# Interleaving the two halves of stationary operands, element by element, for the 512-column matmuls of a two-layer encoder

## The chip, the cores and the metric

The kernel runs on one core of one Trainium2 chip. The metric is device time in microseconds (us) of one launch that computes both outputs. A profile of one execution stands beside the timed runs. Engine names are those of the profile: PE is the matrix engine (its matmuls), PEld the same engine's weight loads, DVE the vector engine, ACT the scalar engine, POOL the general engine, SP the queue that issues most DMAs. L599 is line 599 of the kernel before.

## The reference

Two sequences of 512 tokens with 1024 channels go through the same trunk of two layers. Everything is float32.

```python
for i in range(2):                       # layer 0: attention, layer 1: retention
    h = rms_norm(x, norm_g[i])
    proj = h @ w_in                      # layer 0: 1024 x 8192, layer 1: 1024 x 6144
    q, k, v, gate = split(proj)
    ...
    x = x + (rms_norm(mixer(q, k, v)) * silu(gate)) @ w_out     # 2048 x 1024
y = rms_norm(x, final_norm_g)
```

The attention layer has 8 heads, each with two softmaxes of 512 x 512 scores, subtracted from each other; queries and keys are rotated (rope). The retention layer has 8 heads with a decay in both directions, worked in two chunks of 256 tokens.

## The kernel before, in words

**Halves.** The matmuls take operands in a rounded 32-bit format (fp32r). To keep float32 accuracy each operand is split in two: ACT writes the rounded value (hi, `hi_of`, L399 and L400), DVE writes what is left (lo, `lo_of`, L402 and L403). A product is then three matmuls into one PSUM bank, named by `PASSES`: hi by hi, hi by lo, lo by hi. In each pair the first letter is the stationary operand (the one that PE loads as weights, 128 columns at a time), the second the moving one (streamed through, 512 or 256 columns). Every matmul has its own weight load, also where it loads the same weights as the one before. In the trace a group of three therefore shows six records.

**The input projections.** Both use a seven-product block scheme for matrix products (products P1 to P7, on sums and differences of blocks). A `Unit` covers 256 columns of the weight matrix. In a unit of kind "pair" (queries, keys, gates) the block of the weight matrix is the stationary operand: `prep` makes it (DVE sums and differences into `st`, then hi and lo into a tile of the ring `ws`, which has 7 buffers), and `product` issues 12 matmuls (4 steps of 128 channels by three passes) of 512 columns each at L599, with the moving operands `bt` from the tokens' blocks (`make_b`). In a unit of kind "wide" (values) it is the other way round: token blocks are stationary, the weight matrix moves, 256 columns at a time (L609).

**The tile that a pair product loads.** `prep` takes `ws` as `[P, 2, 4, n]`: all hi values, then all lo values. A load of step k reads 128 values that lie side by side.

**Attention.** Rotated queries and keys leave `rot_done` (its inner `store`) through a staging tile `os` of shape `[P, 2, S]` (row 0 hi, row 1 lo) to DRAM by DMA, and come back through `load_qk`. `scores` (L1104 to L1118) loads 128 queries as weights and moves 512 keys: three matmuls of 512 columns per score tile at L1116. The probabilities are transposed (L1161) and multiplied with the values in matmuls of 256 columns (L1181). `weigh` multiplies by the gate and splits the gated sums into `oT`, two slots of a large tile (`arena`), one for hi and one for lo, made by `new_oT`.

**The output projections.** `out_step` loads 128 tokens of `oT` as weights and moves 512 columns of the output matrix (from `ws`): six matmuls per step at L891. DVE adds the result to the residual (L896). Both layers use it.

**Retention.** Its scores, states and sums are matmuls of 256 columns (L1315, L1339, L1359, L1367).

**What sets the order.** A planner (`Plan`) records every operation with a cost per engine, what it reads and what it writes, simulates the five engines, and fixes one order of instructions per engine when the program is built. At run time each engine follows its list and waits on semaphores.

Of the kernel before, what the change touches and what calls it, by code (L numbers as in the profile page):

```python
# [15 lines left out]
P = 128  # L16
# [237 lines left out]
def trunk_kernel(  # L254
# [45 lines left out]

    arena = ar.tile([P, 18 * 1024 + 80], F32R, tag="arena", name="arena")

    def slot(n, shape, dt=F32R, shift=0):

        size = math.prod(shape[1:])
        at = None if n in (12, 13) or n >= 20 else n if n < 12 else n - 2
        if at is None:
            assert not shift  # L310
            cnt[0] += 1
            label = f"b_{cnt[0]}"
            return Buf(plan, f"b{n}", 1, lambda i: cp.tile(shape, dt, tag=f"b{n}", name=label))
        assert dt == F32R
        lo = 32 + at * 1024 + shift

        def make(i):
            t = arena[:, lo:lo + size]
            return t.rearrange("p (a b) -> p a b", a=shape[1]) if len(shape) == 3 else t
        b = Buf(plan, f"b{n}", 1, make)  # L320
        b.also = Buf(plan, f"edge{at + 1 if shift else at}", 1, None)
        return b
# [195 lines left out]
    class Unit:  # L518
# [32 lines left out]
        def prep(self, op):  # L551
            x = self.take
            n = 256 if self.wide else P

            def combine(a, b, fn):
                t = st_t([P, 4, n])
                out = ((lambda: self.like(t.t)), t)
                dve(4 * n, lambda: nc.vector.tensor_tensor(out[0](), a[0](), b[0](), op=fn), [a[1], b[1]], [t])
                return out
            if op == "P1":  # L560
                src = x(0, 0)
            elif op == "P2":
                src = x(0, 1)
            elif op == "P4":
                src = x(1, 1)
            elif op == "P5":
                src = self.s[1] = combine(x(1, 0), x(1, 1), ALU.add)
            elif op == "P6":
                src = self.s[2] = combine(self.s[1], x(0, 0), ALU.subtract)
            elif op == "P3":  # L570
                src = combine(x(0, 1), self.s[2], ALU.subtract)
            else:
                src = combine(x(0, 0), x(1, 0), ALU.subtract)
            if self.wide:
                a, b = ws_t([P, 4, n]), ws_t([P, 4, n])
                hi, lo = ((lambda: a.t), a), ((lambda: b.t), b)
            else:
                s = ws_t([P, 2, 4, n])
                hi, lo = ((lambda: s[:, 0]), (s, 0)), ((lambda: s[:, 1]), (s, 1))
            hi_of(4 * n, lambda: self.like(hi[0]()), src[0], [src[1]], [hi[1]])  # L580
            lo_of(4 * n, lambda: self.like(lo[0]()), src[0], lambda: self.like(hi[0]()), [src[1], hi[1]], [lo[1]])
            self.ops[op] = (hi, lo)
            if op == "P2" and self.early is not None:
                self.early, self.x = None, {}
# [75 lines left out]
                self.done(1, 0, X, s, True)  # L660


    def rot_done(dst, tab, scaled, turned=None):

        cos, sin = tab

        def mul(out, a, t, psum):
            if scaled:  # L670
                dve(S, lambda: nc.vector.scalar_tensor_tensor(out.t, a.t, SC, t.t, op0=ALU.mult, op1=ALU.mult),
                    [a, t], [out])
            elif psum:
                dve(S, lambda: nc.vector.tensor_tensor(out.t, a.t, t.t, op=ALU.mult), [a, t], [out])
            else:
                dve(S, lambda: nc.vector.tensor_tensor(out.t, a.t, t.t, op=ALU.mult), [a, t], [out])

        def store(g, i, r):
            o = os_t()
            hi_of(S, lambda: o[:, 0, :], lambda: r.t, [r], [(o, 0)])  # L680
            lo_of(S, lambda: o[:, 1, :], lambda: r.t, lambda: o[:, 0, :], [r, (o, 0)], [(o, 1)])
            for j in range(2):
                dma(lambda j=j: dst[g][j, i * 64:(i + 1) * 64], lambda j=j: o[j * 64:(j + 1) * 64].bitcast(F32),
                    [o], [(dst[g], (i, j))], 256)

        def done(i, g, tiles, s, psum):
            x = tiles[0]
            if i == 0:
                s["b0", g] = x
                return  # L690
            a, m1, m2 = s["b0", g], m_t(), m_t()
            mul(m1, a, cos, False)
            mul(a, a, sin, False)
            mul(m2, x, sin, psum)
            if psum:
                m3 = m_t()
                mul(m3, x, cos, psum)
            else:
                m3 = x
                mul(x, x, cos, psum)  # L700
            dve(S, lambda: nc.vector.tensor_tensor(m1.t, m1.t, m2.t, op=ALU.subtract), [m1, m2], [m1])
            store(g, 0, m1)
            dve(S, lambda: nc.vector.tensor_tensor(a.t, a.t, m3.t, op=ALU.add), [a, m3], [a])
            store(g, 1, a)
            if turned:
                turn(g, m1, a)

        def turn(g, *r):
            h, to = turned
            out = [m_t("kt"), m_t("kt")]  # L710
            for i in range(2):
                tp = bank("tp", "ktp")

                def fn(i=i, tp=tp):
                    for t in range(NT):
                        nc.tensor.transpose(tp[:, t * P:(t + 1) * P], r[i][:, t * P:(t + 1) * P], ident.t)
                pe(0.44, fn, [r[i], ident], [tp], 2)
                for j in range(2):
                    dve(256, lambda i=i, j=j, tp=tp: nc.vector.tensor_tensor(
                        out[j].t.rearrange("p (t i c) -> p t i c", t=NT, i=2)[:, :, i, :],  # L720
                        tp.t.rearrange("p (t j c) -> p t j c", t=NT, j=2)[:, :, j, :],
                        powers[:, h + j, :].unsqueeze(2).broadcast_to([P, NT, 64]), op=ALU.mult),
                        [tp, powers], [(out[j], i)])
            for j in range(2):
                o, k = os_t(), out[j]
                hi_of(S, lambda o=o, k=k: o[:, 0, :], lambda k=k: k.t, [k], [(o, 0)])
                lo_of(S, lambda o=o: o[:, 1, :], lambda k=k: k.t, lambda o=o: o[:, 0, :], [k, (o, 0)], [(o, 1)])
                dma(lambda j=j: to[h + j, g].rearrange("a p c -> p a c"), lambda o=o: o.t.bitcast(F32),
                    [o], [to[h + j, g]], 512)
        return done  # L730
# [66 lines left out]
    def weigh(y, sg, oT, c, scale=1.0):  # L797


        here = slice(c * 256, (c + 1) * 256)  # L800
        og, sq = c_t("og"), m_t("sq")
        wide = lambda t: t.rearrange("p (e n) -> p e n", e=2)
        dve(S, lambda: nc.vector.tensor_tensor(wide(og.t), wide(y.t), sg[:, :, here], op=ALU.mult), [y, sg], [og])
        hi_of(S, lambda: oT[0][:, :, here], lambda: wide(og.t), [og], [(oT[0], c)])
        lo_of(S, lambda: oT[1][:, :, here], lambda: wide(og.t), lambda: oT[0][:, :, here], [og, (oT[0], c)],
              [(oT[1], c)])
        act(S, lambda: nc.scalar.activation(sq.t, y.t, AF.Square, scale=scale), [y], [sq])
        dve(256, lambda: nc.vector.tensor_tensor(sq[:, 0:256], sq[:, 0:256], sq[:, 256:512], op=ALU.add), [sq], [sq])
        return sq
# [14 lines left out]
        return rr  # L824

    def new_oT(g):
        return [slot(16 + 2 * g + a, [P, 2, S], F32R, 32) for a in range(2)]

    def load_qk(src, i, shift):
        t = slot(i, [P, 2, S], F32R, shift)  # L830
# [129 lines left out]

    def units1(tab):
        ropes = [Unit(w1, which * DI + h * 256, "pair",
                      rot_done({g: qk_d[0, which, h, g] for g in range(NG)}, tab, which == 0), half_view)
                 for h in range(NH) for which in range(2)]
        gates = [Unit(w1, 3 * DI + h * 256, "pair", gate_done({g: g_d[0, h, g] for g in range(NG)}, 16))
                 for h in range(NH)]
        wides = [Unit(w1, 2 * DI + h * 256, "wide",
                      v_done({(i, g): v_d[0, h + i, g] for i in range(2) for g in range(NG)}))
                 for h in range(0, NH, 2)]
        return mixed(ropes, gates, wides, 2, 5)  # L970
# [136 lines left out]
    def scores(i):  # L1107
        h, g, t = tiles[i]
        st[i]['s'] = []
        for j in range(2):  # L1110
# [2 lines left out]

            def fn(s=s, q=q, k=k):
                for n, (a, b) in enumerate(PASSES):
                    nc.tensor.matmul(s.t, q[:, a, t * P:(t + 1) * P], k[:, b, :], start=(n == 0), stop=(n == 2))  # L1116
            pe(0.7, fn, [q, k], [s])
            st[i]['s'].append(s)  # L1118

# [414 lines left out]
```

## Time and profile before

| | |
|---|---|
| time, median of 3 runs | 1809.73 us (1808.83 to 1810.48) |
| span of the profiled execution, first to last instruction | 1807.0 us |
| median over that span | 2.7 us more |
| granted PE clock, mean | 0.999 |
| POOL busy | 169.5 us (9%) |
| DMA | 328.81 MB moved, mean 182 GB/s |

The profile gives no time of its own for the profiled execution beside the span; the 2.7 us between span and median is taken as what lies around the span. "Busy" is the union of an engine's instructions in time, so that it never exceeds the span. In the groups of instructions a row gives the line, engine, operation, the written tile and the read tiles, the count, the busy time, the mean duration of one record, and the idle time ahead of them. Matmuls are pipelined: a record runs from its start until its results are written, and neighbours overlap, so the mean of one is longer than the distance from one to the next. That distance (the pitch) is found by dividing a stretch of time by the matmuls in it.

### The profile page before, as it was taken

Reading aid. Unit: us, or ns where it says so; the run is one execution under the profiler, and the core shown is the slowest. Engines: PE = TensorE matmul, PEld = TensorE weight load, DVE = VectorE, ACT = ScalarE, POOL = GpSimd, SP = SyncE. Lnnn points to the kernel's source line nnn. Section 1 sums busy time; section 2 is a strip of 40 time slices with the busy share of each in tenths; the row PEclk is TensorE's granted clock in tenths of the full one; section 3 lists DMA queues with packets and bytes.
Section 4 is the critical chain, followed back from the end, with each engine's and each line's share of the span. In section 5 each row is a group of like instructions: output and inputs, shape, how many; then the busy total and the mean of one; then the engine's idle time right before and its main releaser. Section 6 shows DMA issues by size and latency. Waiting matters only on the chain.

```text
span 1807.0 us, 27780 instructions
## 1 busy us (share of the span) xinstructions
PE 1794.9 (99%) x10299; PEld 1558.1 (86%) x10299; DVE 1477.1 (82%) x2319; ACT 895.1 (50%) x1856; POOL 169.5 (9%) x323
## 2 busy tenths in 40 slices
PE   9999999999999999999999999999999999999998
PEld 6789889898988888888888888898989898888887
DVE  7958787778699888888888897787887967888887
ACT  7753444433434565554555866444434355444346
POOL 1000000000000022222322300000000000111113
PEclk9999999999999999999999999999999999999999
DMA  6444455555545685444554524464657559765662
GB/s 217 134 126 137 161 140 178 184 168 155 174 126 175 201 334 198 178 156 159 190 204 140 190 73 146 140 210 146 205 156 228 151 170 396 272 238 182 225 218 94
DMA packets 162767, 328.81 MB, mean 182 GB/s; under 512 B 12724, under 2 KB 76872, under 8 KB 162632
## 3 DMA queue, kind: packets, MB, share of 16 engines
q1 hardware_dynamic: 162304, 326.71, 54.1%
q8 instruction: 81, 1.33, 0.3%
q14 instruction: 54, 0.44, 0.1%
q10 hardware_dynamic: 328, 0.34, 0.1%
HBM read 209.55 MB, written 117.44 MB: 181 GB/s over the span
## 4 chain that ended last, share of the span: by engine, by line
PE 93%; DVE 2%; DMA 2%; ACT 2%; issue 1%; POOL 0%; SPq 0%; POOLq 0%; DVEq 0%; ACTq 0%
PE pj L599 20%; PE pj L891 19%; PE sc L599 10%; PE pj L609 10%; PE o L599 8%; PE o L1181 5%; PE sc L1116 5%; PE sc L609 5%; PE o L609 2%; PE o L1359 2%; PE tp L1161 2%; PE sc L1315 1%; PE o L1367 1%; PE tp L1339 1%; DMA raw<-in_ret_w_out_dram 1%
## 5 line engine op out<-in xcount | busy, mean ns | idle before, releaser
L891 PE MATMUL pj<-ws,arena 128*128 128x512 f32 x1542 | 391.2, 397 | 0.0
L891 PEld LDWEIGHTS pj<-ws,arena 128*128 128x128 f32 x1542 | 277.7, 188 | 52.7
L599 PE MATMUL pj<-b,ws 128*128 128x512 f32 x1080 | 265.0, 392 | 0.0
L599 PEld LDWEIGHTS pj<-b,ws 128*128 128x128 f32 x1080 | 201.4, 188 | 43.0
L403 DVE TENSOR_TENSOR ws<-st,ws 128x512 fp32r<-128x512 f32 (+1 forms) x192 | 147.9, 774 | 74.8 <-ACT ws L400 56.7
L896 DVE SCALAR_TENSOR_TENSOR b<-pj,crr,b 128x512 f32<-128x512 f32 (+1 forms) x257 | 189.9, 744 | 21.4 <-PE pj L891 21.0
L403 DVE TENSOR_TENSOR ws<-raw,ws 128x512 fp32r<-128x512 f32 (+1 forms) x164 | 141.5, 868 | 71.3 <-ACT ws L400 61.0
L400 ACT CAST ws<-st 128x512 fp32r<-128x512 f32 (+1 forms) x192 | 132.4, 693 | 121.4 <-PE pj L599 36.4
L599 PE MATMUL sc<-arena,ws 128*128 128x512 f32 x768 | 186.8, 392 | 0.0
L599 PE MATMUL o<-arena,ws 128*128 128x512 f32 x744 | 180.0, 393 | 1.1 <-ACT m L385 0.6
L599 PEld LDWEIGHTS sc<-arena,ws 128*128 128x128 f32 x768 | 144.0, 188 | 31.3
L400 ACT CAST ws<-raw 128x512 fp32r<-128x512 f32 (+1 forms) x164 | 125.7, 772 | 87.0 <-PE o L599 45.0
L599 PEld LDWEIGHTS o<-arena,ws 128*128 128x128 f32 x744 | 138.4, 188 | 31.7 <-DVE arena L463 1.4
L599 PE MATMUL pj<-arena,ws 128*128 128x512 f32 x648 | 160.3, 392 | 0.4 <-DVE arena L463 0.4
L599 PEld LDWEIGHTS pj<-arena,ws 128*128 128x128 f32 x648 | 120.8, 188 | 26.7 <-DVE arena L463 0.7
L1134 ACT ACTIVATE b<-sc,nm 128x512 f32<-128x512 f32 x128 | 88.0, 689 | 66.9 <-DVE nm L1124 66.5
L636 ACT COPY c<-pj 128x512 f32<-128x512 f32 x104 | 60.9, 586 | 119.7 <-PE pj L599 66.4
L609 PE MATMUL pj<-ws,b 128*128 128x256 f32 x960 | 116.8, 276 | 0.0
L609 PEld LDWEIGHTS pj<-ws,b 128*128 128x128 f32 x960 | 113.2, 188 | 0.7
L1116 PE MATMUL sc<-arena 128*128 128x512 f32 x384 | 101.2, 395 | 0.3 <-ACT b L1134 0.3
L1181 PEld LDWEIGHTS o<-arena 128*128 128x128 f32 x768 | 93.1, 188 | 2.7
L1181 PE MATMUL o<-arena 128*128 128x256 f32 x768 | 93.7, 278 | 0.0
(207 smaller groups left out, 2855.9 us busy)
## 6 DMA issues: line engine op xcount, KB each, us to landing
qk<-os SPq DMA_DIRECT2D x192, 256.0 KB, 3.6
arena<-qk SPq DMA_DIRECT2D x96, 512.0 KB, 5.8
raw<-in_da_w_in_dram SPq DMA_DIRECT2D x64, 512.0 KB, 5.1
v<-os SPq DMA_DIRECT2D x64, 512.0 KB, 4.3
arena<-v SPq DMA_DIRECT2D x64, 512.0 KB, 4.1
raw<-in_ret_w_in_dram SPq DMA_DIRECT2D x48, 512.0 KB, 4.8
os<-g SPq DMA_DIRECT2D x32, 512.0 KB, 7.4
g<-e SPq DMA_DIRECT2D x48, 256.0 KB, 4.6
```

Source lines behind the costliest of these rows:

```text
L400: act(n, lambda: nc.scalar.copy(dst(), src()), r, w)
L403: dve(n, lambda: nc.vector.tensor_tensor(dst(), src(), hi().bitcast(F32), op=ALU.subtract), r, w)
L599: nc.tensor.matmul(ps.t, a[u][0]()[:, k, :], bt[k][:, v, :], start=(opens and k == 0 and i == 0), stop=(k == 3 and i == 2), skip_group_che ...
L609: nc.tensor.matmul(ps[:, (t % 2) * 256:(t % 2) * 256 + 256], bt[k][:, v, t * P:(t + 1) * P], a[u][0]()[:, k, :], start=(opens and t % 2 == ...
L636: act(S, lambda c=c, ps=ps: nc.scalar.copy(c.t, ps.t), [ps], [c])
L891: nc.tensor.matmul(ps[:, here], o[a][:, e, t * P:(t + 1) * P], u[b][:, e, here], start=(m == 0), stop=(m == 5))
L896: axpy(n, lambda half=half, here=here, ps=ps: nc.vector.scalar_tensor_tensor(half, ps[:, here], rr[:, t % 2:t % 2 + 1], half, op0=ALU.mult ...
L1116: nc.tensor.matmul(s.t, q[:, a, t * P:(t + 1) * P], k[:, b, :], start=(n == 0), stop=(n == 2))
L1134: act(840, lambda j=j, s=s, m=m: nc.scalar.activation(p[:, j, :], s.t, AF.Exp, bias=m.t, accum_out=sm[:, 2 * j + n:2 * j + n + 1]), [s, m] ...
L1161: nc.tensor.transpose(tp[:, j * P:(j + 1) * P], p[:, 0, j * P:(j + 1) * P], ident.t)
L1181: nc.tensor.matmul(o[:, e * 256:(e + 1) * 256], v[b][:, j, e * P:(e + 1) * P], aT[a][:, j, :], start=(n == 0), stop=(n % 12 == 11), skip_g ...
L1359: nc.tensor.matmul(o[:, e * 256:(e + 1) * 256], v_[v][:, 2 * c + j, e * P:(e + 1) * P], a_[:, u, j * 256:(j + 1) * 256], start=(e == 0 and ...
```

## The change

Three kinds of stationary operand get another place for hi and lo. They no longer stand in two blocks but alternate, element by element: hi of column 0, lo of column 0, hi of column 1, and so on. A load of 128 hi values then reads every second element over a stretch of 1024 bytes, not 128 neighbours over 512 bytes. The three are the weights of pair products (`prep`), the gated sums (`new_oT`, `weigh`), and the queries of attention (`store`, `scores`). They are just those that a matmul of 512 columns loads. The moving operands and all operands of 256-column matmuls stay as they are. ACT and DVE now write these halves with a step of two elements, and DVE reads hi with that step when it works out lo. The two slots of a gated sum become one stretch, so writing hi counts as a write to both.

```diff
+    def twin(t):
+        return t.rearrange("p a s -> p (a s)").rearrange("p (s u) -> p s u", u=2)
...
-                s = ws_t([P, 2, 4, n])
-                hi, lo = ((lambda: s[:, 0]), (s, 0)), ((lambda: s[:, 1]), (s, 1))
+                s = ws_t([P, 4, n, 2])
+                hi, lo = ((lambda: s[:, :, :, 0]), (s, 0)), ((lambda: s[:, :, :, 1]), (s, 1))
...
-    def rot_done(dst, tab, scaled, turned=None):
+    def rot_done(dst, tab, scaled, turned=None, twins=False):
...
-            hi_of(S, lambda: o[:, 0, :], lambda: r.t, [r], [(o, 0)])
-            lo_of(S, lambda: o[:, 1, :], lambda: r.t, lambda: o[:, 0, :], [r, (o, 0)], [(o, 1)])
+            part = (lambda a: twin(o.t)[:, :, a]) if twins else (lambda a: o[:, a, :])
+            hi_of(S, lambda: part(0), lambda: r.t, [r], [(o, 0)])
+            lo_of(S, lambda: part(1), lambda: r.t, lambda: part(0), [r, (o, 0)], [(o, 1)])
...
-        hi_of(S, lambda: oT[0][:, :, here], lambda: wide(og.t), [og], [(oT[0], c)])
+        hi_of(S, lambda: oT[0][:, :, here], lambda: wide(og.t), [og], [(oT[0], c), (oT[1], c)])
...
     def new_oT(g):
-        return [slot(16 + 2 * g + a, [P, 2, S], F32R, 32) for a in range(2)]
+        both = [slot(16 + 2 * g + a, [P, 2, S], F32R, 32) for a in range(2)]
+        lo = 32 + 32 + (14 + 2 * g) * 1024
+        for a, b in enumerate(both):
+            b.make = lambda i, a=a: arena[:, lo:lo + 2048].rearrange("p (e s u) -> p e s u", e=2, u=2)[:, :, :, a]
+        return both
...
-                      rot_done({g: qk_d[0, which, h, g] for g in range(NG)}, tab, which == 0), half_view)
+                      rot_done({g: qk_d[0, which, h, g] for g in range(NG)}, tab, which == 0, None, which == 0),
+                      half_view)
...
-                    nc.tensor.matmul(s.t, q[:, a, t * P:(t + 1) * P], k[:, b, :], start=(n == 0), stop=(n == 2))
+                    nc.tensor.matmul(s.t, twin(q.t)[:, t * P:(t + 1) * P, a], k[:, b, :], start=(n == 0), stop=(n == 2))
```

## The prediction

> **What bounds the kernel now.** I read the page first, then the list of waits, then the groups of one engine with shapes kept apart, then single stretches. On the page: the span, PE's busy time, and who stands in the chain that ended last.
>
> ```profile
> span 1807.0 us, 27780 instructions
> ...
> PE 1794.9 (99%) x10299; PEld 1558.1 (86%) x10299; DVE 1477.1 (82%) x2319; ACT 895.1 (50%) x1856; POOL 169.5 (9%) x323
> ...
> PE 93%; DVE 2%; DMA 2%; ACT 2%; issue 1%; POOL 0%; SPq 0%; POOLq 0%; DVEq 0%; ACTq 0%
> ```
>
> PE's records cover 99% of the span and PE is 93% of the chain. The waits of PE's matmuls, eight rows in all, of which these are the first and the last, come to about 5 us (1.4 down to 0.2 each).
>
> ```profile
> PE sc L1010 <- DVE minus L411: 1.4, 1, 1.4
> ...
> PE tp L815 <- DVE b L403: 0.2, 1, 0.2
> ```
>
> So nothing is to be had from another engine; the time is the number of matmuls times their pitch. These groups are all the 512-column matmuls that the change touches (columns after the bar: busy us, mean ns of one record, idle).
>
> ```profile
> L891 PE MATMUL pj<-ws,arena 128*128 128x512 f32 x1530 | 389.8, 398 | 0.0
> L599 PE MATMUL pj<-b,ws 128*128 128x512 f32 x1080 | 265.0, 392 | 0.0
> L599 PE MATMUL sc<-arena,ws 128*128 128x512 f32 x768 | 186.8, 392 | 0.0
> L599 PE MATMUL o<-arena,ws 128*128 128x512 f32 x744 | 180.0, 393 | 1.1 <-ACT m L385 0.6 <-DVE arena L463 0.3
> L599 PE MATMUL pj<-arena,ws 128*128 128x512 f32 x648 | 160.3, 392 | 0.4 <-DVE arena L463 0.4
> ...
> L1116 PE MATMUL sc<-arena 128*128 128x512 f32 x384 | 101.2, 395 | 0.3 <-ACT b L1134 0.3
> ...
> L599 PE MATMUL sc<-b,ws 128*128 128x512 f32 x120 | 29.1, 391 | 0.0
> ```
>
> The counts add up to 5274 of PE's 10299 records. Their pitch I take from a stretch with nothing but L599, and beside it a stretch with nothing but 256-column matmuls (L609); columns: PE, PEld, DVE, ACT, POOL busy with counts, granted clock, DMA share, GB/s.
>
> ```profile
> 62.00:150.00 88.00, 88.00 (x386) 72.18 (x386) 67.08 (x106) 50.47 (x85) 0.00 (x0) 1.00 0.43 132
> 163.50:190.60 27.10, 27.10 (x241) 27.10 (x240) 19.25 (x29) 12.03 (x20) 0.00 (x0) 1.00 0.56 172
> ```
>
> A window also counts records that reach into it, one or two here. 88.00 us over 384.5 is 229 ns per 512-column matmul; 27.10 us over 239 is 113.4 ns per 256-column one. At a full clock, then, 5274 x 229 ns = 1208 us, two thirds of the span, is what this change can speed up or slow down. In the second stretch PEld has no gap, so a load of 128 neighbouring values takes at most 113 ns of the load path; in the first it is free for 15.8 of 88 us.
>
> **The change part by part.** The built programs hold the same instructions in the same order on all five engines, before and after, the DMAs included; only 17 lo subtractions lose a wait for PE, because the hi copy ahead of them now makes it. So the planner moves nothing, no queue is passed, and everything lies in how fast the same instructions read and write.
>
> *ACT and DVE.* Pair products are 3360 matmuls (the five L599 rows) at 12 each, 280; with 64 gated sums and 32 query stores that is 376 hi copies and 376 lo subtractions. No row shows a write with a step of two. The nearest rows are reads with that step: in the second layer's rotated units a block of the weight matrix is read so. First all such groups by name, then a stretch in which every copy and subtraction from `raw` reads in steps of two.
>
> ```profile
> L400 ACT CAST ws<-st 128x512 fp32r<-128x512 f32 x160 | 98.7, 621 | 74.9 <-PE pj L599 30.3 <-issue 13.1 <-PE sc L599 11.1
> ```
>
> ```profile
> L403 DVE TENSOR_TENSOR ws<-st,ws 128x512 fp32r<-128x512 f32 x160 | 108.9, 685 | 56.7 <-ACT ws L400 56.2
> ```
>
> ```profile
> L403 DVE TENSOR_TENSOR ws<-raw,ws 128x512 fp32r<-128x512 f32 x3 | 2.1, 689 | 3.2 <-ACT ws L400 3.2
> L400 ACT CAST ws<-raw 128x512 fp32r<-128x512 f32 x3 | 2.0, 651 | 1.4 <-PE sc L599 1.4
> ```
>
> ACT pays 651 - 621 = 30 ns, DVE 689 - 685 = 4 ns. As an estimate for writes: 376 x 30 ns = 11 us more on ACT, which is busy half the time, and 376 x 4 ns = 1.5 us on DVE. What hides them is PE's own backlog: it waits 5 us in the whole run. Without that cover they would cost at most 13 us together. Below nothing they can't go by more than those 5 us. I take 0.
>
> *The loads themselves.* No row shows a load in steps of two. The largest group of loads now:
>
> ```profile
> L891 PEld LDWEIGHTS pj<-ws,arena 128*128 128x128 f32 x1542 | 277.7, 188 | 52.7
> ```
>
> The step matters in two ways: how long the load takes, and what it does to the matmul that streams beside it. For the length, one end is no change; the other is twice, 226 ns, since twice the bytes are spanned. Even that fits the 229 ns pitch by 3 ns. It would only be seen at the head of a run, where a matmul waits for its own load:
>
> ```profile
> L891 PE MATMUL pj<-ws,arena 128*128 128x512 f32 x1 | 0.5, 477 | 0.0
> ```
>
> That is one head, 477 ns where a steady record has 392: 85 ns of waiting. L891's mean of 398 says (398 - 392) x 1530 / 85 = 108 heads, L1116's 395 another 14. At 113 ns more each, a doubled load costs 122 x 113 ns = 14 us. I take no change.
>
> For the neighbour, the trace has a matmul that ran with no load beside it: the load path was idle for 0.57 us until 50.27, while the second of these two matmuls streamed from 49.73 on.
>
> ```profile
> 49.73 1.04 PE L599 MATMUL o<-arena,ws 128*128 128x512 f32 x2
> 50.27 0.19 PEld L599 LDWEIGHTS o<-arena,ws 128*128 128x128 f32 x1 [0.57 <-DVE arena L463]
> ```
>
> ```profile
> L599 PE MATMUL o<-arena,ws 128*128 128x512 f32 x1 | 0.4, 388 | 0.0
> ```
>
> It took 388 ns, where records with a load beside them take 391 to 393. I read the 4 ns as what a load and a stream cost each other when they want the same part of SBUF. The two walk at different speeds now: the stream passes 2048 bytes per partition in 229 ns, 8.9 bytes per ns, a load 512 bytes in 113 ns, 4.5. Whatever their start, they fall in and out of step. With a step of two a load passes 1024 bytes in 113 ns, 9.1 bytes per ns: the stream's own speed. Side by side at a constant distance, they either never want the same place or always do. The tiles' places put every such load 64 bytes off its stream, counted modulo 128, and a load starts with its neighbour's stream, so I take "never".
>
> The sum: 4 ns x 5274 = 21 us (the same 4 ns for L891 and L1116, whose means hold the heads). 1807.0 - 21 = 1786 us of span, 2.7 us around it as in the median of the runs: **1789 us**. What is late next is still PE.
>
> [...]
>
> **The rivals.**
> 1. *No contention to remove.* The 4 ns come from something else (the end of a run, say), and the load has slack as it is. Speaking for it: 388 is one record of its kind, and the pitch is the same 229 ns whichever tiles are read. The time is 1810 us, with up to 4 more for ACT's 11 us where its results are awaited. [...]
> 2. *Always in step, on the wrong side.* The constant distance is one at which load and stream collide at each line, for instance because the load's data are asked for earlier or later than its record starts. Now they meet about half of the time for 4 ns; always would be 8: +21 us, 1831 us, spread over L599, L891 and L1116 alike. It decides as soon as the colliding share is over a half. Against it: the 64 bytes.
> 3. *A longer load.* At twice its length 1824 us, by the heads alone (L891). From 229 ns on, 2.02 times the present length, every matmul waits: each further 10 ns cost 53 us. Against it: on ACT and DVE the step of two cost 5% and 1%, not 100%.
> [...]
>
> **How the numbers follow.** Forecast (never in step) 0.42; rival 4 0.10; rival 1 0.16; rival 2 0.22; rival 3 0.10, of which 0.04 lie beyond a doubled load. Faster by over 0.2% (about what a measurement of this kernel can tell from no change, 3.6 us) 0.52, within it 0.16, slower 0.32. The forecast's own range is 1782 to 1800. With both signs likely, the whole range reaches from 1765, some way into what lies between the forecast and rival 4, to just over rival 2, 1835: left out are most of rival 4 and the far part of rival 3, about 0.15.
>
> **What would show it.** Right: in a pure L599 stretch the pitch falls from 229 to 225 ns, the records' mean from 392 to 388, the 256-column stretch stays at 113.4 ns, and PE's waits stay near 5 us. Rival 1: 392 stays. Rival 2: 396 and a pitch of 233. Rival 3: PEld's mean above 188 ns, heads above 477. [...] ACT's copies at about 650 ns would confirm the side cost; DVE subtractions far above 689 ns, with new DVE rows among PE's waits, would show that I hid too much. A change of the 256-column pitch would put the whole picture in doubt, since no operand of theirs is touched.

## The result and the profile after

The changed kernel takes 1841.38 us (median of 5 runs, 1840.45 to 1841.5) against 1809.73: a ratio of 1.0175, 95% interval 1.0162 to 1.0187. It is slower, on the other side of the forecast of 1789, and 6.4 us above the upper end of the range. Three lines from the page of the changed kernel: the span, the busy times, the chain that ended last.

```profile
span 1839.5 us, 27771 instructions
...
PE 1827.6 (99%) x10299; PEld 1607.6 (87%) x10299; DVE 1480.1 (80%) x2319; ACT 907.6 (49%) x1856; POOL 170.4 (9%) x323
...
PE 93%; DMA 3%; DVE 2%; ACT 1%; issue 0%; POOL 0%; SPq 0%; POOLq 0%
```

The picture is as before: as many matmuls, 99% of the span, 93% of the chain. PE is busy 32.7 us longer and the span is 32.5 us longer. PE waits for nobody more than before: of its eight waits by line, these are the first and the last (total, times, longest, in us), and all eight come to 4.5 us.

```profile
PE sc L1021 <- DVE minus L415: 1.4, 1, 1.4
...
PE sc L1127 <- ACT b L1145: 0.3, 1, 0.3
```

So the same matmuls in the same order run at a longer pitch. The groups of 512-column matmuls (L603, L901 and L1127 were L599, L891 and L1116):

```profile
L901 PE MATMUL pj<-ws,arena 128*128 128x512 f32 x1530 | 394.2, 401 | 0.0
L603 PE MATMUL pj<-b,ws 128*128 128x512 f32 x1080 | 269.4, 396 | 0.0
L603 PE MATMUL sc<-arena,ws 128*128 128x512 f32 x768 | 190.1, 396 | 0.0
L603 PE MATMUL o<-arena,ws 128*128 128x512 f32 x744 | 183.2, 397 | 1.1 <-ACT m L389 0.6 <-DVE arena L467 0.3
L603 PE MATMUL pj<-arena,ws 128*128 128x512 f32 x648 | 163.1, 396 | 0.4 <-DVE arena L467 0.3
...
L1127 PE MATMUL sc<-arena 128*128 128x512 f32 x384 | 102.4, 398 | 0.3 <-ACT b L1145 0.3
```

Each mean is 3 to 4 ns above its old one (398, 392, 392, 393, 392, 395). That much the prediction had as its second rival. But the 256-column matmuls, of which no operand was touched, are slower as well; first before, then after.

```profile
L609 PE MATMUL pj<-ws,b 128*128 128x256 f32 x960 | 116.8, 276 | 0.0
...
L609 PE MATMUL sc<-ws,arena 128*128 128x256 f32 x768 | 89.6, 276 | 0.0
...
L1359 PE MATMUL o<-arena 128*128 128x256 f32 x384 | 48.9, 276 | 0.0
```

```profile
L613 PE MATMUL pj<-ws,b 128*128 128x256 f32 x960 | 120.9, 281 | 0.0
...
L613 PE MATMUL sc<-ws,arena 128*128 128x256 f32 x768 | 93.1, 281 | 0.0
...
L1370 PE MATMUL o<-arena 128*128 128x256 f32 x384 | 50.3, 280 | 0.0
```

Two stretches of the changed kernel, one with nothing but L603 and one with nothing but L613 (PE, PEld, DVE, ACT, POOL with counts, clock, DMA share, GB/s):

```profile
62.00:150.00 88.00, 88.00 (x379) 73.55 (x378) 65.43 (x104) 49.93 (x82) 0.00 (x0) 1.00 0.42 130
168.00:193.00 25.00, 25.00 (x214) 25.00 (x213) 16.25 (x25) 10.07 (x16) 0.00 (x0) 1.00 0.47 151
```

Counted as in the prediction, 88.00 us over 377.5 is 233 ns (it was 229), and 25.00 us over 212 is 118 ns (it was 113.4), both at a full clock. From here on a pitch is the distance from the end of one matmul's record to the end of the next, averaged over a group without the gaps at its heads; "sum" is the sum of all these distances in a group, gaps included. Both are taken from the trace's records. By them the span's growth divides so:

| group | matmuls | sum before, us | sum after, us | more | pitch, ns |
|---|---|---|---|---|---|
| pair products, 512 columns | 3360 | 772.7 | 787.0 | 14.3 | 229.0 to 233.3 |
| output projections, 512 | 1530 | 353.0 | 357.4 | 4.4 | 230.6 to 233.5 |
| attention's scores, 512 | 384 | 89.1 | 90.3 | 1.2 | 230.0 to 233.1 |
| wide products, 256 (untouched) | 2688 | 305.4 | 316.0 | 10.6 | 113.6 to 117.6 |
| attention's and retention's other matmuls, 256 (untouched) | 1728 | 199.4 | 202.5 | 3.1 | |

The 512-column groups give 19.9 us, the untouched ones 13.7; matmuls of 128 columns give back 0.5. The sum, 33.1 us, is the growth of the distance from the first matmul after the warm-up to the last (1788.5 to 1821.5 us); the warm-up itself was 0.6 us shorter, which leaves the span's 32.5.

### The profile page after: what moved, and what is told of

It is laid out like the page before. It is cut to its first block, busy times and chain, and to the rows that moved or that the text cites. A ratio compares the mean times of both kernels' runs of the same rounds, so it can differ in the third digit from the quotient of the medians.

```text
span 1839.5 us, 27771 instructions
## 1 busy us (share of the span) xinstructions
PE 1827.6 (99%) x10299; PEld 1607.6 (87%) x10299; DVE 1480.1 (80%) x2319; ACT 907.6 (49%) x1856; POOL 170.4 (9%) x323
## 4 chain that ended last, share of the span: by engine, by line
PE 93%; DMA 3%; DVE 2%; ACT 1%; issue 0%; POOL 0%; SPq 0%; POOLq 0%
PE pj L603 20%; PE pj L901 19%; PE sc L603 11%; PE pj L613 10%; PE o L603 8%; PE sc L613 5%; PE o L1192 5%; PE sc L1127 5%; PE o L613 2%; PE o L1370 2%; PE tp L1172 2%; PE o L1378 1%; PE sc L1326 1%; PE tp L1350 1%; DMA raw<-in_ret_w_out_dram 1%; DMA raw<-in_da_w_in_dram 1%
## 5 line engine op out<-in xcount | busy, mean ns | idle before, releaser
L901 PE MATMUL pj<-ws,arena 128*128 128x512 f32 x1542 | 395.6, 400 | 0.0
L901 PEld LDWEIGHTS pj<-ws,arena 128*128 128x128 f32 x1542 | 288.2, 195 | 46.8
L603 PE MATMUL pj<-b,ws 128*128 128x512 f32 x1080 | 269.4, 396 | 0.0
L603 PEld LDWEIGHTS pj<-b,ws 128*128 128x128 f32 x1080 | 209.1, 195 | 40.0
L404 ACT CAST ws<-st 128x512 fp32r<-128x512 f32 (+1 forms) x192 | 138.6, 726 | 134.9 <-PE pj L603 41.0
L603 PE MATMUL sc<-arena,ws 128*128 128x512 f32 x768 | 190.1, 396 | 0.0
L603 PE MATMUL o<-arena,ws 128*128 128x512 f32 x744 | 183.2, 397 | 1.1 <-ACT m L389 0.6
L404 ACT CAST ws<-raw 128x512 fp32r<-128x512 f32 (+1 forms) x164 | 129.6, 796 | 94.0 <-PE o L603 42.4
L603 PEld LDWEIGHTS sc<-arena,ws 128*128 128x128 f32 x768 | 149.5, 195 | 29.2
L603 PEld LDWEIGHTS o<-arena,ws 128*128 128x128 f32 x744 | 143.6, 195 | 29.6 <-DVE arena L467 1.3
L603 PE MATMUL pj<-arena,ws 128*128 128x512 f32 x648 | 163.1, 396 | 0.4 <-DVE arena L467 0.3
L603 PEld LDWEIGHTS pj<-arena,ws 128*128 128x128 f32 x648 | 125.4, 195 | 24.9 <-DVE arena L467 0.6
L613 PE MATMUL pj<-ws,b 128*128 128x256 f32 x960 | 120.9, 281 | 0.0
L613 PEld LDWEIGHTS pj<-ws,b 128*128 128x128 f32 x960 | 117.1, 189 | 0.6
L1127 PE MATMUL sc<-arena 128*128 128x512 f32 x384 | 102.4, 398 | 0.3 <-ACT b L1145 0.3
```

The lines of the kernel that those rows point to most:

```text
L404: act(n, lambda: nc.scalar.copy(dst(), src()), r, w)
L603: nc.tensor.matmul(ps.t, a[u][0]()[:, k, :], bt[k][:, v, :], start=(opens and k == 0 and i == 0), stop=(k == 3 and i == 2), skip_group_che ...
L613: nc.tensor.matmul(ps[:, (t % 2) * 256:(t % 2) * 256 + 256], bt[k][:, v, t * P:(t + 1) * P], a[u][0]()[:, k, :], start=(opens and t % 2 == ...
L901: nc.tensor.matmul(ps[:, here], o[a][:, e, t * P:(t + 1) * P], u[b][:, e, here], start=(m == 0), stop=(m == 5))
L1127: nc.tensor.matmul(s.t, twin(q.t)[:, t * P:(t + 1) * P, a], k[:, b, :], start=(n == 0), stop=(n == 2))
```

## The experiments

The reference time of each set is the kernel before on the same chip, 1808.56 to 1809.95 us. A distance below is the first byte of the weights that a load reads, less the first byte of the stream in progress (the next matmul's weights beside the present matmul's moving operand), in bytes of a partition counted modulo 512. It comes from the addresses in the built program. The pair products of both kernels stand at 192, which is the prediction's 64 modulo 128.

### One part at a time

`e1_pair` interleaves the weights of pair products alone, `e2_sums_queries` the gated sums and the queries alone.

```diff
-                s = ws_t([P, 2, 4, n])
-                hi, lo = ((lambda: s[:, 0]), (s, 0)), ((lambda: s[:, 1]), (s, 1))
+                s = ws_t([P, 4, n, 2])
+                hi, lo = ((lambda: s[:, :, :, 0]), (s, 0)), ((lambda: s[:, :, :, 1]), (s, 1))
```

> Only the weights of pair products are interleaved (L599, 3360 matmuls); gated sums and queries stay in blocks. Theory A (the load): a load in steps of two costs the matmul that streams beside it about 4.3 ns, wherever such a load runs and nowhere else; the slower 256-column matmuls are an after-effect of the state in which a run of them is entered. Then the pure L599 stretch has a pitch of 233.3 ns against 228.9, L891 and L1116 keep theirs, and the time is 1809.7 + 14.3 = 1824 us, up to 1836 if the 256-column runs of the projections fall into the slow state too. Theory B (the writes): stepped writes of ACT and DVE slow all of PE's reads while they run; with 280 of 376 such writes the time is about 1833 us, and L891 and L1116 are slower where such writes run beside them.

> The complement: gated sums and queries interleaved, pair products' weights in blocks. Theory A: L891 and L1116 go to a pitch of about 233.3 ns (from 230.6 and 230.0), 1530 x 2.9 + 384 x 3.1 = 5.6 us more, 1815 us, and the projections' 256-column runs keep 113.4 ns; L599 stays at 228.9. Theory B: 96 of 376 writes, about a quarter of the loss, 1818 us, and the projections keep their time.

e1 took 1832.82 us, 1.0125 (1.0108 to 1.0142); e2 took 1817.23 us, 1.0040 (1.0027 to 1.0054). Together that is 23.7 + 8.1 = 31.8 us, the whole loss of the changed kernel (31.7 us). In e1 only the pair products go to 233.3 ns; output projections and scores stay at 230.6 and 230.2. In e2 it is the other way round: 233.5 and 233.2, pair products at 229.05. So the 512-column part follows the loads that are changed, and only these. The 256-column part doesn't: in e1 the wide products are at 117.2 ns, in e2 at 113.7, but there the retention's untouched matmuls (L1359 and L1367 of before) are at 117.6 and 117.7.

### The writes or the loads

The change alters the way the halves are written and the way they are loaded. `e5_writes` writes them interleaved, as e1 does, but loads 128 neighbours; `e6_loads` writes blocks, as before, and loads every second element.

```diff
-                            ps.t, a[u][0]()[:, k, :], bt[k][:, v, :], ...
+                            ps.t, load(k, u), bt[k][:, v, :], ...
# e5, on an interleaved ws:      at = 256 * k + 128 * u;  load = w[:, at:at + 128]
# e6, on a ws in two blocks:     at = 256 * k + u;        load = w[:, at:at + 255:2]
```

> Pair products' weights are written interleaved by ACT and DVE as in e1_pair, but each load reads 128 neighbouring elements, so it mixes hi and lo of 64 columns: these products are not the reference's. Theory A: pitch 228.9 ns, time 1810 us within 3. Theory B: the time of e1_pair, 1824 to 1836 us.

> The reverse: written in blocks as before, but each load of a pair product reads every second element over 1024 bytes, so it mixes channels: these products are not the reference's. Theory A: the pitch and the time of e1_pair, 1824 to 1836 us. Theory B: 1810 us within 3.

e5: 1810.22 us, 1.0001 (0.9992 to 1.0011). e6: 1833.2 us, 1.0126 (1.0106 to 1.0146). A matmul group and a load group of e5, then the same of e6:

```profile
L606 PE MATMUL pj<-b,ws 128*128 128x512 f32 x1080 | 265.0, 392 | 0.0
```

```profile
L606 PEld LDWEIGHTS pj<-b,ws 128*128 128x128 f32 x1080 | 201.5, 188 | 43.0
```

```profile
L606 PE MATMUL pj<-b,ws 128*128 128x512 f32 x1080 | 269.4, 396 | 0.0
```

```profile
L606 PEld LDWEIGHTS pj<-b,ws 128*128 128x128 f32 x1080 | 209.1, 195 | 40.0
```

With interleaved writes and plain loads nothing changes; with plain writes and stepped loads everything of e1 is there. The writes are out: it is the load. Its own record grows from 188 to 195 ns, and the matmul beside it from 392 to 396.

### Is it the load's length?

`e8_step4`, `e12_step3` and `e11_step0` load in steps of four, three and none (one element, 128 times).

```diff
# e8:   at = 512 * (k % 2) + 2 * (k // 2) + u;  load = w[:, at:at + 509:4]
# e12:  at = 128 * k + u;                       load = w[:, at:at + 382:3]
# e11:  at = 512 * u + 128 * k;                 load = w[:, at:at + 1].broadcast_to([P, 128])
```

> Weights in blocks as before, but the loads of pair products read every fourth element over 2048 bytes; they mix halves and channels, so these products are not the reference's. Theory A2: the extra of 4.3 ns grows with the stretch touched: twice as many bytes again, so 229 + 4.3 + 8.6 = 242 ns, and a mean load record near 209 ns, 1809 + 13 x 3.36 = 1853 us and up to 12 more by the wide runs. Theory A1: the load now walks at twice the stream's speed and falls out of step, so the pitch falls back to about 229.

> Weights in blocks, loads of pair products in steps of three elements (12 bytes); they mix halves and channels, so these products are not the reference's. [...]

> Weights in blocks as before, but each load of a pair product reads one and the same element 128 times (step 0); these products are not the reference's. It measures what a load of 128 neighbours costs the stream at all. The prediction's step (a lone matmul took 388 ns, one with a load beside it 392): if a load's reads collide with the stream, a load that touches one place only brings the pitch to about 225 ns, 1809 - 13 = 1796 us. If the 4 ns were not a collision: 229 ns and 1809 us.

They took 1846.61, 1831.2 and 1816.19 us (one run each). The load group of e8, of e12 and of e11:

```profile
L606 PEld LDWEIGHTS pj<-b,ws 128*128 128x128 f32 x1080 | 265.9, 312 | 0.1
```

```profile
L606 PEld LDWEIGHTS pj<-b,ws 128*128 128x128 f32 x1080 | 254.8, 252 | 0.1
```

```profile
L606 PEld LDWEIGHTS pj<-b,ws 128*128 128x128 f32 x1080 | 201.6, 188 | 45.1
```

| step of the load | 0 | 1 | 2 | 3 | 4 |
|---|---|---|---|---|---|
| load record, ns | 188 | 188 | 195 | 252 | 312 |
| pitch of pair products, ns | 231.3 | 229.0 | 233.3 | 235.4 | 239.6 |
| wide products, ns | 113.5 | 113.6 | 117.5 | 113.6 | 113.6 |

Length does count where it is long: at steps of three and four the load path has no gap left (0.1 us idle). At two it has (40.0 us), and the pitch is 4.3 ns up nevertheless, so length is not the reason there.

e11 speaks against the forecast's own reason, without settling it. A load of one element, 128 times, stays at one place, and the pitch is 231.3 ns, above the 229.0 of the plain load, where the forecast's reason had led me to expect 225. But the stream still passes that place, and only one place was tried.

### Is it the place?

`e7_flip` moves e1's stepped loads by 64 bytes, later for the first three steps, earlier for the last; `e10_flip_blocks` does the same with plain loads. `e17_sweep_blocks` and `e18_sweep_step2` give each of the seven products a place of its own. All of them load other values than the product wants.

```diff
# e7:   at = 256 * k + u + (16 if k < 3 else -16);        load = w[:, at:at + 255:2]
# e10:  at = 512 * u + 128 * k + (16 if k < 3 else -16);  load = w[:, at:at + 128]
# d = dict(P1=0, P2=16, P5=32, P6=64, P3=80, P7=96, P4=112)[op]
# e17:  at = 512 * u + 128 * min(k, 2) + d;               load = w[:, at:at + 128]
# e18:  at = 256 * min(k, 2) + u + d;                     load = w[:, at:at + 255:2]
```

> As e1_pair (pair products' weights written interleaved, loads in steps of two), but each load starts 16 elements (64 bytes) later, or earlier in the last of four steps, so that load and stream lie at the other distance modulo 128 bytes; the loads mix channels, so these products are not the reference's. Theory A1 (in step: load and stream walk side by side, and the constant distance decides whether they collide): the pitch of L599 leaves 233.3 ns, down to 225 if they now never meet. Theory A2 (the load itself takes longer and the stream pays for each stretch of bytes the load touches, at any distance): 233.3 ns as in e1_pair.

> The kernel before with one edit: each load of a pair product reads 128 neighbours that start 64 bytes later (earlier in the last step), so load and stream lie at the other distance modulo 128 bytes; these products are not the reference's. If the distance mattered for block loads, the pitch of L599 leaves 229 ns (by up to 4 ns, 13 us); if loads and streams do not collide by place, which e7_flip and e11_step0 suggest, 229 ns and 1810 us.

> The kernel before with the block loads of pair products started at another distance for each of the seven products (P1 0, P2 64, P5 128, P6 256, P3 320, P7 384, P4 448 bytes later, so 192, 256, 320, 448, 0, 64 and 128 bytes from the stream modulo 512); they read the wrong columns, so these products are not the reference's. Theory P: each product has its own pitch, 228.9 ns at 192, 226.7 at 256, most at 0 or 128 (235 and more). Without it all seven have 229.

> The same seven distances with loads in steps of two. If a stepped load walks beside the stream at a constant distance and that distance decided (rival 2 of the prediction), the products differ: about 225 at some distances, well above 233 at others. If the step itself costs the 4.3 ns, all seven have 233.3.

They took 1833.81, 1813.47, 1821.55 and 1824.94 us (one run each). In e7 the pair products stand at 256, and in the last step at 128; their pitch is 233.4 ns, as in e1, which by itself looked as if the place were of no account. In e10 the pitch is 226.9 ns where the distance is steadily 256, about 2 ns better than the kernel before; the whole is slower all the same, since the last step stands at 128, and over all pair products the pitch is 230.6 ns. For the two sweeps I took matmuls whose four forerunners stand at the same distance (275 to 328 for each place):

| distance, bytes | 0 | 64 | 128 | 192 | 256 | 320 | 448 |
|---|---|---|---|---|---|---|---|
| plain loads (e17), ns | 227.1 | 233.3 | 233.0 | 228.7 | 227.2 | 233.3 | 228.7 |
| loads in steps of two (e18), ns | 233.3 | 230.1 | 231.4 | 233.3 | 233.5 | 230.3 | 233.3 |

The pitch of 512-column matmuls depends on the place of the load relative to the stream, also with plain loads, by 6 ns (e17). As far as measured it repeats after 256 bytes: 0 and 256, 64 and 320, 192 and 448 agree within 0.2 ns. The two curves run against each other: where plain loads are cheap, stepped ones are dear. The kernel's pair products stand at 192, where plain loads have 228.7 and stepped ones 233.3, within 0.2 of their worst. The best that a stepped load reaches, 230.1, is still above what the kernel has now.

### The same two kernels at other places

If that is so, the verdict on the change hangs on the place. `e15_base16` and `e16_after_base16` put the arena, which holds the streams of two thirds of the pair products, 64 bytes lower in the kernel before and in the changed one; `e19_base0` and `e20_after_base0` put it 128 bytes lower. The computation stays the reference's.

```diff
-        lo = 32 + at * 1024 + shift
+        lo = 16 + at * 1024 + shift      # e15, e16;  e19, e20: lo = at * 1024 + shift
# in e16 and e20 also new_oT's own start, 16 + 32 + ... and 32 + ... for 32 + 32 + ...
```

> The kernel before, everything in blocks, with one number changed: all slots of the arena start 16 elements (64 bytes) earlier, so that loads from ws and streams from the arena lie 256 bytes apart modulo 512, not 192. In e10_flip_blocks the triples of matmuls at 256 ran at 226.7 ns, those at 128 near 235. Theory P (the distance modulo 512 bytes sets the pitch of block loads): the 2160 L599 matmuls that stream from the arena go from 228.9 to 226.7 ns, -4.8 us, 1805 us; the 1200 that stream from outside it keep 228.9; L891, whose loads move by -64 bytes against their stream, and the wide products change by a few ns either way. If the distance is of no account and e10's pattern came from its irregular steps: 1809.7 us.

> The changed kernel with the same shift of the arena's slots by 64 bytes. Theory P holds for block loads alone if a load in steps of two keeps its distance to the stream and was at neither of the two distances tried so far (e1_pair, e7_flip) free of the 4.3 ns: then L599 stays at 233.3 ns and the time at 1841 us, unless the wide runs are entered in another state, which can take off up to 12 us. If stepped loads follow the distance too, the pitch of the 2160 matmuls from the arena leaves 233.3.

> The kernel before, all in blocks, with the slots of the arena 128 bytes earlier: loads from ws and streams from the arena now lie 320 bytes apart modulo 512. By the table of e17_sweep_blocks the 2160 L599 matmuls that stream from the arena go from 228.9 to 233.3 ns (+9.5 us), the other 1200 keep theirs. Loads and streams of the wide products and of L891 move by 128 bytes as well, and no run has measured them there; with no change in them 1819 us.

> The changed kernel with the same shift. By the table of e18_sweep_step2 stepped loads at 320 run at 230.3 ns, so the 2160 matmuls go from 233.3 to 230.3 ns (-6.5 us) and are 3 ns faster than the same matmuls of e19_base0, where at 192 they were 4.4 ns slower: the verdict on interleaving these weights turns round with the place. The other 1200 keep 233.3. With L901 and the wide runs unchanged 1835 us. If the distance were of no account for stepped loads, 233.3 ns and 1841 us.

| kernel | us | ratio to before | pair pitch by distance, ns | wide, ns |
|---|---|---|---|---|
| e15, blocks | 1832.01 | 1.0119 (1.0103 to 1.0134) | 256: 227.9, 192: 228.8 | 119.2 |
| e16, interleaved | 1843.92 | 1.0185 (1.0167 to 1.0203) | 256: 233.3, 192: 233.3 | 119.2 |
| e19, blocks | 1827.11 | 1.0097 (1.0080 to 1.0114) | 320: 233.3, 192: 229.5 | 115.3 |
| e20, interleaved | 1826.86 | 1.0098 (1.0083 to 1.0113) | 320: 230.0, 192: 233.2 | 115.2 |

Two groups of pair products in e19 and the same two in e20. The first streams from `b`, whose distance stays at 192; the second from the arena, now at 320.

```profile
L599 PE MATMUL pj<-b,ws 128*128 128x512 f32 x1080 | 265.5, 393 | 0.0
L599 PE MATMUL sc<-arena,ws 128*128 128x512 f32 x768 | 190.1, 396 | 0.0
```

```profile
L603 PE MATMUL pj<-b,ws 128*128 128x512 f32 x1080 | 269.4, 396 | 0.0
L603 PE MATMUL sc<-arena,ws 128*128 128x512 f32 x768 | 187.7, 393 | 0.0
```

At 192 the change costs 3 ns of record, at 320 it gains 3 ns. Both gain and loss can be set by moving the streams, and with the arena 128 bytes lower the two kernels are level (1827.11 and 1826.86). That settles the part of the pair products. The output projections, which load from the arena, go the same way: with the arena 128 bytes lower most of them stand at 320, not 448, and they have 233.0 ns in blocks (e19) and 231.5 interleaved (e20), where it was 230.6 and 233.5. For attention's scores the distance is not the whole story. Their loads and streams both lie in the arena, so that it stays at 448, and in blocks they go from 230.0 ns to 231.8 (e15) and 232.1 (e19); no run shows why.

As a better version neither place serves: the pair products of e15 do go to 227.9 ns where they stand at 256, but its wide products go to 119.2 ns (320.4 us for 305.4) and its output projections from 230.6 to 232.2, at distances that were not swept for them.

### Where the untouched 256-column matmuls lose

As long as the arena stays where it is, all their loads stand at a distance of 320, and their pitch has two values. In the kernel before, all 24 stretches of wide products of 36 to 240 matmuls run at 113.4 to 113.8 ns. In the changed one 20 of them run at 117.8 from start to end, and only the four of 36 matmuls, which follow four transposes on PE (L721), run at 113.5. The very first stretch follows four transposes too (L610) and runs at 117.8. `e9_lead_in` is the changed kernel with one idle transpose ahead of the first wide matmul of products P1 and P2, 15 in all.

```diff
+                elif op in ("P1", "P2") and t == 0:
+                    nc.tensor.transpose(ps[:, 0:P], ident.t, ident.t)
```

> The changed kernel with one idle transpose (109 ns) ahead of products P1 and P2 of each wide unit but the first product of all, 15 in all, so that these runs of 256-column matmuls are entered in another phase. If the 117.8 ns pitch is a state that a run keeps from its entry on, some or all of these runs go to 113.4 ns; the longest gain, for all runs of 48 and 240, is 2304 x 4.3 = 10 us less 1.6 for the transposes, 1833 us. If the pitch comes from something that lasts (memory traffic, the clock), nothing changes but 1.6 us more, 1843 us.

It took 1835.62 us (one run), 5.8 us less than the changed kernel; the sum of the 2688 wide matmuls falls from 316.0 to 308.0 us, and the 15 transposes take 1.6 of that back. Three stretches of e9: the first unit's, the second unit's, and the short stretch after the second, which has no transpose ahead of it.

```profile
168.00:193.00 25.00, 25.00 (x214) 25.00 (x213) 16.14 (x25) 9.59 (x16) 0.00 (x0) 1.00 0.49 150
305.00:330.00 25.00, 25.00 (x223) 25.00 (x222) 16.65 (x26) 10.21 (x17) 0.00 (x0) 1.00 0.50 153
335.00:339.00 4.00, 4.00 (x36) 4.00 (x36) 1.39 (x2) 0.69 (x2) 0.00 (x0) 1.00 0.58 195
```

The middle one passes 9 matmuls more in the same 25 us: 113.4 ns against 117.8. Seven of the eight 240-matmul stretches changed over; that of the first unit did not, although it has the transpose too. The three 48-matmul stretches that got one as well now run at 113.6. All eight stretches that end a unit, with no transpose ahead, stayed at 117.8 or 117.9. So at this distance a stretch takes one of the two paces early (in the kernel before, the stretches of 240 run at 113 to 114 ns after four distances of 116 to 122) and keeps it for up to 240 matmuls; what stands ahead of it turned seven of the eight stretches of 240 in e9, not the first.

The place of the loads matters here too. In e15, where all loads are plain, wide matmuls whose load stands at 256 run at 119.9 ns and those at 320 at 117.9. In e19 each of the eight 240-matmul stretches has about 96 matmuls at 192 first, at 117.7 or 117.8 ns, and goes over to 113.4 where loads at 320 come in between.

That the stepped load is not itself the cause shows in e8 and e12 (steps of four and three, wide products at 113.6), and in the next two. `e13_cols384` and `e14_cols384_step2` cut 3240 of the pair products' matmuls to 384 columns, with plain loads and with loads in steps of two, and so leave a part of the computation out.

```diff
-                            ps.t, a[u][0]()[:, k, :], bt[k][:, v, :], ...
+                            ps[:, 0:n_of(k, i)], load(k, u), bt[k][:, v, 0:n_of(k, i)], ...
# n_of: 512 for a product's first matmul that opens a bank, else 384
# e13:  load = w[:, at:at + 128];   e14:  load = w[:, at:at + 255:2]
```

> The kernel before with 384 columns, not 512, in 3240 of the 3360 matmuls of pair products (the first of each bank keeps 512), block loads; a quarter of these products is left out, so they are not the reference's. [...]

> As e13_cols384 with loads in steps of two. If the 4.3 ns are paid once per load, they come again in full beside a shorter stream: the pitch of e13_cols384 + 4.3 ns. If they are paid by the column, + 3.2 ns. If the load (195 ns, of which about 115 hold the load path) becomes the bound, far more.

e13 took 1717.23 us, e14 1701.8 (one run each, and PE now waits for DVE and ACT; the granted clock is 0.987 and 0.991). The median pitch of the 384-column matmuls is 173 ns in both: at this width, and at the one place tried, a step of two costs nothing. A 256-column group of e13, with no stepped load in the kernel, and the same of e14:

```profile
L619 PE MATMUL pj<-ws,b 128*128 128x256 f32 x960 | 120.9, 281 | 0.0
```

```profile
L619 PE MATMUL pj<-ws,b 128*128 128x256 f32 x960 | 116.8, 276 | 0.4 <-DVE e L654 0.4
```

Here it is the kernel with plain loads whose wide products run at 117.5 ns, and the one with stepped loads at 113.6. That alone is about 10 of the 15.4 us between them. In the kernel before, too, the slower pace exists: attention's matmuls at L1181, in stretches of 24, have some at 113.6 and some at 117.9.

## Why the prediction was wrong, point by point

**Bound and order of work: right.** PE stayed the bound, its waits stayed near 5 us, the order of instructions is the same.

**ACT and DVE: right.** The hi copy and the lo subtraction of the pair products' weights in the changed kernel:

```profile
L404 ACT CAST ws<-st 128x512 fp32r<-128x512 f32 x160 | 104.9, 661 | 83.5 <-PE pj L603 33.9 <-issue 13.2 <-PE sc L603 11.5
```

```profile
L407 DVE TENSOR_TENSOR ws<-st,ws 128x512 fp32r<-128x512 f32 x160 | 109.2, 686 | 60.9 <-ACT ws L404 60.8
```

The copy takes 661 ns for 621, 40 more where I took 30 from the stepped reads; the subtraction 686 for 685. ACT's busy time grew by 12.5 us (I had 11) and I see none of it at the end: e5 has the 280 of 376 such copies and subtractions that belong to pair products, and the time of before; for the other 96, PE's waits are no longer than they were.

**The load's length: right.** It grew by 7 ns, from 188 to 195, and stayed inside the pitch. The third rival falls.

**The failed step: "I take 'never'", and with it the saving of 4 ns x 5274.** In place of 4 ns less, the pair products' pitch grew by 4.3 ns, the output projections' by 2.9 and the scores' by 3.1. The step has three parts, and each fell. For the first, a row of the trace of before: the 120 matmuls of one L599 group, all with a load beside them (shortest, median and longest record, in ns).

```profile
L599 PE MATMUL sc<-b,ws x120: 388/392/394, 94.3 to 1135.7; 128*128 128x512 f32 x120
```

1. *388 against 392 ns as the price of a collision that a load can avoid.* That set one record against a mean, and the row above refutes it. L599's records come in a beat of three, 388, 392 and 394 ns, and 1061 of the 3360 are 388 long. The lone record (the first of the two shown in the prediction, not the second) stood just where the beat had its 388: the three ahead of it, each with a load beside it, have 388, 392 and 394. Six more 512-column matmuls of that trace have no load beside them, and five of them take 396 or 397 ns. So the trace has no sign that a stream without a load is faster, and the forecast's 4 ns per matmul was not there to be saved. The runs at other places agree: none brought the pitch to 225 ns, neither with plain loads (226.9 at best) nor in steps of two (230.1).
2. *"Whatever their start, they fall in and out of step"*, so that plain loads would cost the same at every place. e17 has 227.1 to 233.3 ns for plain loads. The kernel's tiles stand near the good end of that, and I took their 229 ns for a mean. That the pitch was the same "whichever tiles are read" had a simpler reason: the pair products all stand at one distance, 192.
3. *64 bytes modulo 128 as a safe distance for a stepped load.* At 192 modulo 512 stepped loads have 233.3 ns, their worst value but for 0.2. Counting modulo 128, in halves, was an estimate of mine that no row showed; the sweep shows a repeat after 256, with another shape.

The size and sign of rival 2 came out instead: +21 us, a pitch of 233 and records of 396, against +19.9 us, 233.3 and 396. Its reason, a constant distance on the wrong side, is the right one in kind; but the side depends on the place (e19 and e20), and the gap between the sides is not the same for plain and stepped loads (6.2 ns in e17, 3.4 in e18). Its size was twice the 4 ns of the misread record, so that it came so close is in part luck. Rival 1 falls with its number, but its doubt about the 388 was right. For rival 4, which stands in the chances and in the range as a saving beyond the forecast's, no run shows the term: the lowest pitch of 512-column matmuls is 226.9 ns (e10), 2.1 below the 229.0 of the kernel before.

**What no case held: 13.7 us in matmuls that the change does not touch.** The prediction named a change of the 256-column pitch as what would put its picture in doubt, and gave it no chance. It is the reason why the time lies above 1835, the end of the range: 1807.0 + 19.9 + 2.7 gives 1829.6 without it. The trace of before could have warned: L1181 shows both paces there.

**What stays open.** Why the pitch depends on the distance modulo 256 (e17, e18), and why plain and stepped loads do so in opposite ways; why a step of two costs nothing at 384 columns; and what decides which pace a stretch of 256-column matmuls takes. e9 shows that what stands ahead of a stretch can decide it, and e19 that a pace can change within a stretch where the distances change, but neither shows by what. A version better than the kernel before was not found. Moving only the pair products' loads to a distance of 0 or 256, with all other places kept, would save about 1.6 ns x 3360 = 5 us, an estimate from e17's 227.1 against its 228.7 at 192; it needs 64 bytes more in each `ws` tile and was not tried.

## What to carry to other kernels

Here PE's matmuls filled 99% of the span, and the change of layout came out as a change of pitch, 229.0 to 233.3 ns for the pair products. So measure the pitch of one stretch with the new access first, at the distance between weights and stream that the tiles really have, and at two or three others, before a sum over thousands of matmuls is made from one record. Set such a record against the spread of the ordinary ones, not against their mean: here a third of them had its length. Look at the shapes that the change does not touch as well, stretch by stretch: here the 256-column ones had two paces, 113.4 and 117.8 ns, and the change tipped them. And a verdict such as "interleaving costs 1.75%" holds for one placement of the tiles; here a shift of 128 bytes made it zero (1827.11 and 1826.86 us, e19 and e20), at a price elsewhere.

## What the runs showed of the hardware beyond that

- The pitch of 512-column matmuls of this format, each with its own load, lies between 226.9 and 233.5 ns at a granted clock of 0.999 for the pair products with loads in steps of one and two, by the place of the load relative to the stream and the load's step (e10, e17, e18).
- Wide matmuls of 256 columns whose loads all stand at 320 have two paces, 113.4 and 117.8 ns, and keep one for a whole stretch of up to 240 (before, after, e9). At 256 they run at 119.9 (e15), and where loads at 192 give way to a mix with 320 they go from 117.8 to 113.4 within a stretch (e19).
- In the kernel before, L599's records with a load beside them come in a beat of 388, 392 and 394 ns; the seven 512-column matmuls with none have 388 or 396 to 397.
- Weight loads of 128 four-byte values take 188, 188, 195, 252 and 312 ns by their records at steps of 0 to 4 (e11, before, e6, e12, e8).
- At 384 columns the median pitch is 173 ns with plain loads and with steps of two (e13, e14).
